# Half of the low weight parts made by ScalarE and an adding DMA instead of VectorE

## Chip, core and metric

The kernel runs on one core of one Trainium2 chip. The metric is the device time of one execution in microseconds; less is better. It is compared with the kernel before, timed on the same chip.

## What is computed

A trunk of two decoder layers over 256 tokens of width 2048, all in float32. Layer 0 mixes tokens with gated linear attention beside block attention, layer 1 with forgetting attention beside a gated recurrence. After each mixer comes an output projection and a wide MLP. Almost all arithmetic is in products of 256 rows with large weight matrices:

```python
u = rms_norm(h, norm_mix) @ w_in                    # 2048 x 6160 (layer 0), 2048 x 7176 (layer 1)
h = h + concat(mixer_a(u), mixer_b(u)) @ w_out      # 2048 x 2048
h = h + square(relu(rms_norm(h, norm_mlp) @ w_up)) @ w_down   # 2048 x 8192, 8192 x 2048
...
return rms_norm(h, final_norm)
```

## The kernel before

The big products are cut into blocks of 1024 output columns (a few of 1040 or 1032), and each block into 16 units. A unit is one weight tile of 128 rows by 1024 columns with the matmuls that use it. There are 784 units: 16 for each of 49 blocks (6 input, 2 output and 16 MLP blocks in layer 0; 7, 2 and 16 in layer 1).

TensorE multiplies in float32r, which keeps fewer bits than float32. So each operand is split in two: a high part, the value rounded to float32r, and a low part, what is left. `fetch(i)` prepares unit i: a load on SP's queue brings the raw tiles of two units at once (1 MB, line 972), ScalarE copies the raw tile into `wh` (line 978), and VectorE subtracts, `wl = raw - wh` (line 979). The raw tiles lie in three buffers of two units each (pool `wraw`); `wh` and `wl` have six buffers each, one per unit (pool `wspl`).

`step(t, i)` issues the six matmuls of unit i for token half t: activations high times `wh` (two banks), high times `wl` (two banks), low times `wh` (two banks), line 1006. The main loop runs over i: fetch(i + AHEAD), step(0, i), some background work of the mixers (transposes, small products, elementwise work, cut in pieces by `bg`), and step(1, i - LAG), with LAG = 2. A scheduler in the build may move instructions on an engine's queue as dependences allow; in the first 14 iterations `pin` holds the program's order. Each engine then works its own queue off in order, and the hardware waits only where a semaphore says so.

So the buffers of unit k become free when step(1, k - 6) has read them, which is in iteration k - 4. The first matmul of unit k is in iteration k. Between lie iterations k - 3, k - 2 and k - 1, whatever AHEAD is.

GpSimd has little work: masks, the reciprocal roots of the norms (lines 241 to 247) and a few copies. At the start it issues eight small loads (lines 142 to 147).

Of the kernel before, what the change touches and what calls it, by code (L numbers as in the profile page):

```python
# [8 lines left out]
F32 = mybir.dt.float32  # L9
# [11 lines left out]
LAG = 2  # L21
AHEAD = 2
STARTN = 14
# [14 lines left out]
def trunk(ctx: ExitStack, tc: tile.TileContext, x, ev_norm_mix, ev_w_in, ev_gla_gate_w2, ev_gla_gate_b,  # L38
# [10 lines left out]

# [1 line left out]
    # A task yields what its piece costs, or BAR: go on after the next step only.  # L51
    tasks = []
# [32 lines left out]

    # Buffers that tasks take and give back
    def aux():
# [22 lines left out]

# [1 line left out]
    h = cons.tile([P, 2, D], F32, name="h")  # L112
# [5 lines left out]

# [1 line left out]
    vrow0 = work.tile([16, P], F32, name="vrow0", tag="lev", bufs=NLEV)  # L120
# [41 lines left out]
    masks = {}  # L162
    # key - query distance, with the causal mask: columns [queries 0..127 | queries 128..255]
    dist = cons.tile([P, 384], F32, name="dist")
# [7 lines left out]
    def const_task():  # L172
        # tri[s, t] = 1 for s <= t < 128 and for t >= 128
        pool.memset(tri, 1.0)
        pool.affine_select(out=tri[:, 0:P], in_=tri[:, 0:P], pattern=[[1, P]], compare_op=ALU.is_ge, fill=0.0, base=0,
                           channel_multiplier=-1)
        pool.memset(seg, 1.0)
        pool.memset(seg.rearrange("p (a b) -> p a b", b=64)[:, :, 0:1], 0.0)
        for m in LEVELS[1:]:
            yield from room(0, 1)  # L180
            nb = 64 // m
            mf = lev()[:, 0:64]
            mk = cons.tile([P, 256], U8, name=f"mask{m}")
            mv = mf.rearrange("p (n m) -> p n m", m=m) if 1 < m < 64 else mf
            dims = [[2 * m, nb]] * (nb > 1) + [[0, m]] * (m > 1)
            pool.memset(mf, 1.0)
            pool.affine_select(out=mv, in_=mv, pattern=[[-a, b] for a, b in dims], compare_op=ALU.is_ge, fill=0.0,
                               base=0, channel_multiplier=1)
            pool.affine_select(out=mv, in_=mv, pattern=dims, compare_op=ALU.is_ge, fill=0.0, base=m - 1,
                               channel_multiplier=-1)  # L190
            yield BAR
            dve.tensor_copy(mk.rearrange("p (g c) -> p g c", c=64), mf.unsqueeze(1).to_broadcast([P, 4, 64]))
            lev_done()
            masks[m] = mk
            yield 0.3
        pool.iota(dist[:, 0:128], pattern=[[1, 128]], base=0, channel_multiplier=-1,
                  allow_small_or_imprecise_dtypes=True)
        pool.iota(dist[:, 128:384], pattern=[[1, 256]], base=-128, channel_multiplier=-1,
                  allow_small_or_imprecise_dtypes=True)
        causal(dist)  # L200
        yield BAR
        mx, e0, e1, sm = (small([P, 8], f"lb{i}", 1) for i in range(4))
        dve.tensor_tensor(mx, vec("lb0"), vec("lb1"), ALU.max)
        dve.tensor_sub(e0, vec("lb0"), mx)
        dve.tensor_sub(e1, vec("lb1"), mx)
        act.activation(e0, e0, AF.Exp)
        act.activation(e1, e1, AF.Exp)
        dve.tensor_add(sm, e0, e1)
        dve.reciprocal(sm, sm)
        dve.tensor_mul(e0, e0, sm)  # L210
        dve.tensor_mul(e1, e1, sm)
        dve.tensor_add(lb, e0, e1)
        dve.tensor_sub(lb, lb, e0)
        yield 1.0

# [1 line left out]
    xh = cons.tile([P, KT, S], F32R, name="xh")  # L217
# [9 lines left out]

# [1 line left out]
    ssq = {}  # L229
# [9 lines left out]
    def rsq(dst, v, n, scale):  # L239
        """dst = (v * scale + EPS) ** -0.5"""  # L240
        pool.tensor_scalar(dst, v, scale, EPS, ALU.mult, ALU.add)
        pool.tensor_tensor(dst, dst, mhalf[:, 0:n], ALU.pow)
# [8 lines left out]
    def pin(op):  # L251
        """In the first units each engine goes by the order of the program"""
        if state["start"]:
            tc.keep_in_program_order(op)
# [34 lines left out]

# [1 line left out]
    def evac_scaled(dst, acc, sc):  # L291
# [3 lines left out]
    def evac_extra(dst, accs, sc, extra, few, sf):  # L295
        """few <- the extra columns; dst <- the 1024 others"""
        a, b, c = accs
        n = 512 - extra
        m = n + b.shape[1]
        act.activation(dst[:, 0:n], a[:, extra:512], AF.Identity, scale=sc)  # L300
        dve.tensor_scalar(dst[:, n:m], b, sc, None, ALU.mult)
        dve.tensor_scalar(dst[:, m:1024], c, sc, None, ALU.mult)
        act.activation(few, a[:, 0:extra], AF.Identity, scale=sf)

    def silu_gen(z):
        """z = x / 2 -> x * sigmoid(x) = (1 + tanh(x / 2)) * x / 2"""
        for i in range(2):
# [9 lines left out]
    def heads_gen(src, n0, n, dst, t, func=AF.Copy, scale=1.0):  # L317
        """dst[:, 0:n, t] <- transposes of src's blocks n0.. (four at most)"""
        yield from room(1)
# [12 lines left out]

# [1 line left out]
    def spawn_scores(store, qT, kT, bT, escale, h0, diag, *needs):  # L334
        """Heads h0, h0+1. store[h0] = diag [key, (head tile), query], off [key, head, query].
        diag: [token, (head tile)] of q . k, if it's there already."""
        hs = slice(h0, h0 + 2)
# [100 lines left out]
    def gla_out(at, v, g, dv, h0, nh, k0, gain, halves, key):  # L438
        """Outputs of nh heads (nh * dv = 256) from head h0 on; k tiles k0, k0+1 of the half"""
        yield from room(1)  # L440
# [50 lines left out]

# [1 line left out]
    def soft_scores(pts, qT, kT, hd, bias_gen):  # L493
        """Leaves normalized probabilities, transposed [key, query]."""
        yield from room(2, 1)
# [59 lines left out]

# [1 line left out]
    class Block:  # L557
        def __init__(self, w, c0, rows, stat, evac, budget, ready, extra=0):
            """extra: so many columns before the 1024; the products are then in three banks."""
            self.w, self.c0, self.rows, self.stat, self.evac = w, c0, rows, stat, evac  # L560
# [3 lines left out]

# [1 line left out]
    def mixers(lay):  # L566
# [31 lines left out]

        # GLA
        def gla_qk(acc, t):  # L600
# [64 lines left out]

        # HGRN2
        def hg_q(acc, t):
# [5 lines left out]
            sg = stage()  # L673
            # the forget logits of FoX come with the queries
            evac_extra(sg, acc, st["rh"][:, t:t + 1], 8, st["fn"][:, t], st["r"][:, t:t + 1])
# [24 lines left out]
        def hg_gates():  # L700
            """e = exp(-z): log f = ln(1 + lb e) - ln(1 + e), k = 1 - f, b = running sums of log f"""
            b, k = st["b"], st["k"]
# [32 lines left out]

        # MoBA, FoX
        def soft_q(acc, t):
# [9 lines left out]
            else:  # L747
                # the low-rank gates of GLA come with the queries
                evac_extra(sg, acc, st["rq"][:, t:t + 1], 16, st["few"][:, t], st["r"][:, t:t + 1])
# [21 lines left out]
        def fox_forget():  # L771
            """ct = running sums of log sigmoid, token by token; nc = the same, negative, as rows"""
            z = st["fn"]
# [60 lines left out]
    def layer_blocks(lay):  # L834
# [17 lines left out]
        for half in range(2):  # L852
            # the stationary operands come mixer by mixer: its rows of the weights are order[j]
            bl.append(Block((w_out[0], order), half * CB, list(range(KT)), mstat, out_evac(half), 2.0, mready))
# [103 lines left out]

# [1 line left out]
    split, raws, accs = {}, {}, {}  # L960
    blocks, units = [], []

    def fetch(i):
# [14 lines left out]
        pin(act.activation(wh, raw, AF.Copy))  # L978
        pin(dve.tensor_sub(wl, raw, wh.bitcast(F32)))  # L979
        split[i] = (wh, wl)  # L980

    def step(t, i, end=None):
        """Step i, or steps i to end, the last ones of a block, bank by bank"""
        b, j = units[i]
# [17 lines left out]
        outs = list(zip(banks, b.cuts))  # L1002
        # bank by bank in the first and the last step, as the banks come and go one by one
        order = [(o, p) for o in outs for p in parts] if j in (0, n - 1) and i else [(o, p) for p in parts for o in outs]
# [6 lines left out]

    # first loads and transposes
    tk_const = Task(const_task())
# [68 lines left out]
```

## Time and profile before

| | |
|---|---|
| time, median of 2 runs | 2354.7 us (2353.91 to 2355.49) |
| span of the profiled execution, first to last instruction | 2351.9 us |
| what lies around the span, against that median | 2.8 us |
| TensorE matmul busy | 2333.3 us, 99% |
| VectorE busy | 1302.3 us, 55% |
| ScalarE busy | 1067.2 us, 45% |
| GpSimd busy | 61.7 us, 3% |
| read from HBM | 414.47 MB |

PE is TensorE's matmuls, PEld its weight loads, DVE VectorE, ACT ScalarE, POOL GpSimd, SP the engine that issues most loads; a name with q is an engine's queue of DMA issues. Busy time is the union of an engine's instructions. Matmuls overlap in the pipeline, so the sum of their single durations is more than the busy time.

### The profile page before, as it was taken

The page shows a single profiled execution, that of the slowest core. Times are in us where ns is not written, and L with a number is a line of the kernel's source. Part 1 is how long each engine was busy: PE and PEld are TensorE (multiplying, and loading weights), DVE is VectorE, ACT ScalarE, POOL GpSimd, SP SyncE. Part 2 cuts the span into 40 slices and gives each one's busy share as a digit, 9 for nine tenths or more (in the row PEclk, how much of TensorE's full clock was granted, in tenths as well). Part 3 has the DMA queues.
Part 4 walks back from the last instruction along what each step waited for, and adds up shares of the span by engine and source line. Part 5 has one row for each costly group of instructions (what it writes and reads, how often), then busy time and mean ns, then how long its engine had stood idle before and what let it go on. Part 6 is the DMA issues. An engine that isn't in the chain of part 4 may idle for free.

```text
span 2351.9 us, 27073 instructions
## 1 busy us (share of the span) xinstructions
PE 2333.3 (99%) x10836; PEld 1910.8 (81%) x10836; DVE 1302.3 (55%) x1595; ACT 1067.2 (45%) x1334; POOL 61.7 (3%) x126
## 2 busy tenths in 40 slices
PE   8999999999999999999999999999999999999998
PEld 7888888888888888888887888788888888888886
DVE  5485555554554554465557775555554554554554
ACT  5464544443443343344446455544443443443443
POOL 3000200000000000000000000100000000000000
PEclk9999999999999999999999999999999999999999
DMA  7545445555555555555554444455555555555553
GB/s 242 191 155 160 158 156 187 182 184 182 194 179 185 190 179 191 186 180 181 186 182 165 150 139 161 144 179 181 187 187 183 189 182 189 187 179 194 182 180 124
DMA packets 110590, 418.31 MB, mean 178 GB/s; under 512 B 6815, under 2 KB 8945, under 8 KB 110337
## 3 DMA queue, kind: packets, MB, share of 16 engines
q1 hardware_dynamic: 109536, 415.46, 53.6%
q8 instruction: 85, 1.39, 0.2%
q10 hardware_dynamic: 608, 1.06, 0.1%
q14 instruction: 41, 0.33, 0.0%
q0 software_dynamic: 320, 0.07, 0.0%
HBM read 414.47 MB, written 2.10 MB: 177 GB/s over the span
## 4 chain that ended last, share of the span: by engine, by line
PE 98%; DVE 1%; ACT 1%; DMA 0%; SPq 0%; issue 0%; POOL 0%; POOLq 0%; ACTq 0%
PE acc L1006 90%; PE aux L421 1%; PE aux L881 1%; PE aux L1006 1%; PE aux L260 1%; PE aux L322 1%; DMA raw<-in_ev_w_in_dram 0%; PE aux L499 0%; DVE hb L721 0%; PE aux L523 0%; PE aux L805 0%; ACT wh L978 0%; DVE wl L979 0%; PE aux L498 0%; PE aux L414 0%; PE aux L544 0%
## 5 line engine op out<-in xcount | busy, mean ns | idle before, releaser
L979 DVE TENSOR_TENSOR wl<-raw,wh 128x1024 fp32r<-128x1024 f32 (+2 forms) x784 | 959.7, 1225 | 919.2 <-ACT wh L978 918.8
L978 ACT ACTIVATE wh<-raw 128x1024 fp32r<-128x1024 f32 (+2 forms) x784 | 830.4, 1061 | 1169.3 <-PE acc L1006 1091.1
L1006 PE MATMUL acc<-wh,xh 128*128 128x512 f32 x1856 | 605.5, 396 | 2.5 <-ACT xh L266 2.5
L1006 PE MATMUL acc<-wl,xh 128*128 128x512 f32 x1856 | 591.8, 390 | 2.6 <-DVE wl L979 2.6
L1006 PE MATMUL acc<-wh,xl 128*128 128x512 f32 x1856 | 591.3, 389 | 0.0
L1006 PE MATMUL acc<-wh,mh 128*128 128x512 f32 x1280 | 418.2, 396 | 0.0
L1006 PE MATMUL acc<-wl,mh 128*128 128x512 f32 x1280 | 413.5, 394 | 0.0
L1006 PE MATMUL acc<-wh,ml 128*128 128x512 f32 x1280 | 412.9, 393 | 0.0
L1006 PEld LDWEIGHTS acc<-wl,xh 128*128 128x128 f32 x1856 | 344.9, 188 | 78.3 <-DVE wl L979 4.4
L1006 PEld LDWEIGHTS acc<-wh,xl 128*128 128x128 f32 x1856 | 345.3, 188 | 75.1
L1006 PEld LDWEIGHTS acc<-wh,xh 128*128 128x128 f32 x1856 | 339.0, 188 | 73.1 <-ACT xh L266 3.4
L1006 PEld LDWEIGHTS acc<-wl,mh 128*128 128x128 f32 x1280 | 240.5, 188 | 56.0
L1006 PEld LDWEIGHTS acc<-wh,ml 128*128 128x128 f32 x1280 | 240.3, 188 | 56.1
L1006 PEld LDWEIGHTS acc<-wh,mh 128*128 128x128 f32 x1280 | 239.0, 188 | 54.7 <-DVE h L843 1.5
L843 DVE TENSOR_TENSOR h<-acc,h 128x512 f32<-128x512 f32 x72 | 47.8, 685 | 21.0 <-PE acc L1006 21.0
L399 ACT ACTIVATE lev<-lev 128x512 f32<-128x512 f32 x48 | 29.8, 629 | 31.1 <-DVE lev L394 10.9
L875 DVE TENSOR_TENSOR stg<-stg 128x512 f32<-128x512 f32 x64 | 42.6, 686 | 2.4 <-ACT stg L866 1.5
L886 DVE TENSOR_TENSOR ml<-aux,mh 128x512 fp32r<-128x512 f32 x64 | 41.0, 682 | 0.0
L421 PEld LDWEIGHTS aux<-lev 128*128 128x128 f32 x288 | 36.7, 191 | 2.6
L881 PE MATMUL aux<-ident,stg 128*128 128x128 f32 x256 | 36.2, 274 | 0.0
L421 PE MATMUL aux<-lev 128*128 128x64 f32 x288 | 35.8, 269 | 0.0
L881 PEld LDWEIGHTS aux<-ident,stg 128*128 128x128 f32 x256 | 29.6, 140 | 6.6
(229 smaller groups left out, 862.4 us busy)
## 6 DMA issues: line engine op xcount, KB each, us to landing
raw<-in_ev_w_up_dram SPq DMA_DIRECT2D x64, 1024.0 KB, 5.1
raw<-in_ev_w_down_dram SPq DMA_DIRECT2D x64, 1024.0 KB, 5.1
raw<-in_od_w_up_dram SPq DMA_DIRECT2D x64, 1024.0 KB, 5.0
raw<-in_od_w_down_dram SPq DMA_DIRECT2D x64, 1024.0 KB, 5.1
raw<-in_od_w_in_dram SPq DMA_DIRECT2D x48, 1024.0 KB, 4.9
raw<-in_ev_w_in_dram SPq DMA_DIRECT2D x39, 1024.0 KB, 5.4
raw<-in_ev_w_out_dram SPq DMA_DIRECT2D x16, 1024.0 KB, 5.1
raw<-in_od_w_out_dram SPq DMA_DIRECT2D x16, 1024.0 KB, 5.1
```

What stands on the lines that cost most here:

```text
L260: pin(pe.transpose(ps[:, i * 256 + t * P:i * 256 + (t + 1) * P], h[:, t, kt * P:(kt + 1) * P], ident))
L322: pe.transpose(ps[:, i * P:(i + 1) * P], src[:, (n0 + i) * P:(n0 + i + 1) * P], ident)
L399: act.activation(e, e, AF.Exp, scale=escale)
L421: pe.matmul(ps[:, i * 64:(i + 1) * 64], a, r, start=True, stop=True)
L843: dve.tensor_tensor(h[:, t, sl], acc[i], h[:, t, sl], ALU.add)
L875: dve.tensor_tensor(sg[:, cs], sg[:, cs], sg[:, cs], ALU.mult)
L881: pe.transpose(ps[:, j * P:(j + 1) * P], sg[:, i * 512 + j * P:i * 512 + (j + 1) * P], ident)
L886: dve.tensor_sub(ml[:, ks, ts], pv, mh[:, ks, ts].bitcast(F32))
L978: pin(act.activation(wh, raw, AF.Copy))
L979: pin(dve.tensor_sub(wl, raw, wh.bitcast(F32)))
L1006: pin(pe.matmul(o, a, m[:, c0:c1], start=first, stop=last))
```

## The change

From unit 32 on, the units whose number leaves 2 or 3 when divided by 4 get their low part in another way. ScalarE writes `-raw`, rounded to float32r, into `wl`, and a DMA of GpSimd's queue then adds the raw tile to it. The subtraction on VectorE is left out for these units. There are 376 of them, always both units of one raw buffer, and the two units before and after stay as they were. AHEAD becomes 3. The number of buffers stays. All else in the diff are comments that became empty lines.

```diff
-AHEAD = 2
+AHEAD = 3
...
         wh = wspl.tile([P, n], F32R, name="wh", tag="wh")
         wl = wspl.tile([P, n], F32R, name="wl", tag="wl")
         pin(act.activation(wh, raw, AF.Copy))
-        pin(dve.tensor_sub(wl, raw, wh.bitcast(F32)))
+        if i >= 32 and i % 4 >= 2:
+
+            act.activation(wl, raw, AF.Copy, scale=-1.0)
+            pool.dma_start(out=wl, in_=raw, accum_op=ALU.add)
+        else:
+            pin(dve.tensor_sub(wl, raw, wh.bitcast(F32)))
         split[i] = (wh, wl)
```

## Rows read from the trace of the kernel before

**Rows 1.** The page's head and busy times.

```profile
span 2351.9 us, 27073 instructions
...
PE 2333.3 (99%) x10836; PEld 1910.8 (81%) x10836; DVE 1302.3 (55%) x1595; ACT 1067.2 (45%) x1334; POOL 61.7 (3%) x126
```

**Rows 2.** Who waited for whom, all engines: total us, times, longest.

```profile
ACT wh L978 <- PE acc L1006: 1091.1, 655, 5.2
POOL rstd L247 <- ACT stg L235: 997.6, 4, 726.8
...
ACT stg L866 <- PE acc L1006: 14.7, 16, 0.9
...
PEld acc L1006 <- DVE wl L979: 4.4, 4, 2.6
...
PE acc L1006 <- DVE wl L979: 2.6, 3, 2.1
```

**Rows 3.** The page's costliest groups: the two instructions of the split.

```profile
L979 DVE TENSOR_TENSOR wl<-raw,wh 128x1024 fp32r<-128x1024 f32 (+2 forms) x784 | 959.7, 1225 | 919.2 <-ACT wh L978 918.8
L978 ACT ACTIVATE wh<-raw 128x1024 fp32r<-128x1024 f32 (+2 forms) x784 | 830.4, 1061 | 1169.3 <-PE acc L1006 1091.1
```

**Rows 4.** Timeline of ScalarE near the end: start, duration, idle before and releaser.

```profile
2325.63 1.06 ACT L978 ACTIVATE wh<-raw 128x1024 fp32r<-128x1024 f32 x1 [1.73 <-PE acc L1006]
2328.41 1.06 ACT L978 ACTIVATE wh<-raw 128x1024 fp32r<-128x1024 f32 x1 [1.72 <-PE acc L1006]
```

**Rows 5.** Timeline of TensorE near the end.

```profile
2333.79 0.63 PE L1006 MATMUL acc<-wh,mh 128*128 128x512 f32 x2
2334.26 0.63 PE L1006 MATMUL acc<-wl,mh 128*128 128x512 f32 x2
```

**Rows 6.** Busy time by stage: stretch, length, busy times, clock, DMA share, GB/s.

```profile
0.00:300.00 300.00, 293.48 (x1474) 244.52 (x1475) 181.94 (x314) 159.05 (x241) 34.72 (x71) 1.00 0.56 180
300.00:392.00 92.00, 92.00 (x437) 75.83 (x436) 47.38 (x53) 41.80 (x53) 0.00 (x0) 1.00 0.53 172
392.00:1120.00 728.00, 728.00 (x3231) 591.83 (x3230) 386.97 (x384) 306.89 (x328) 1.11 (x3) 1.00 0.56 185
1120.00:1488.00 368.00, 365.57 (x1891) 304.72 (x1890) 232.89 (x371) 193.57 (x293) 20.31 (x38) 1.00 0.48 161
1488.00:1592.00 104.00, 104.00 (x496) 84.50 (x495) 53.83 (x79) 51.54 (x80) 2.97 (x8) 1.00 0.53 172
```

**Rows 7.** Timeline inside an MLP block: a split and what hands over.

```profile
700.98 1.06 ACT L978 ACTIVATE wh<-raw 128x1024 fp32r<-128x1024 f32 x1 [1.74 <-PE acc L1006]
...
702.08 1.22 DVE L979 TENSOR_TENSOR wl<-raw,wh 128x1024 fp32r<-128x1024 f32 x1 [1.57 <-ACT wh L978]
```

**Rows 8.** DMA issues: count, KB each, median us from issue to landing.

```profile
raw<-in_ev_w_up_dram SPq DMA_DIRECT2D x64, 1024.0 KB, 5.1
...
out_dram<-lev ACTq DMA_DIRECT2D x2, 256.0 KB, 2.8
...
vrow<-in_ev_norm_mlp_dram POOLq DMA_DIRECT2D x1, 8.0 KB, 6.1
...
fb<-in_od_fox_fgate_b_dram POOLq DMA_DIRECT2D x1, 4.0 KB, 5.0
```

**Rows 9.** GpSimd's groups: its own time for one DMA issue.

```profile
L147 POOL DMA_DIRECT2D fb<-in_od_fox_fgate_b_dram x1 | 0.6, 574 | 1.7 <-DMA vrow<-in_ev_norm_mlp_dram 1.7
```

**Rows 10.** DMA queues: packets, MB, share of the 16 engines' span.

```profile
q1 hardware_dynamic: 109536, 415.46, 53.6%
```

**Rows 11.** The loads of one matrix: duration of an issue, first and last start.

```profile
L972 SPq DMA_DIRECT2D raw<-in_od_w_down_dram x64: 367/368/368, 1685.2 to 2314.1; - x64
```

## The prediction

> **What bounds the kernel now.** I read the busy times first: TensorE's matmuls cover 2333.3 of 2351.9 us [rows 1], and the granted clock is 1.00 in every stage [rows 6]. So at most 18.6 us of the span are without a matmul, and no change that leaves the matmuls alone can give more. The view of waits says what little TensorE waits for: `wl` from VectorE costs it 2.6 us as a matmul and 4.4 us as a weight load, 7 us in all [rows 2]. ScalarE by contrast waits 1091.1 us, 655 times, to write `wh`, for a matmul to give the buffer back [rows 2]. The split is therefore early everywhere: it starts the moment a buffer is free. What counts is then how much time lies between that moment and the matmul that needs the result; nothing else of the change can reach the end of the kernel.
>
> **The cover.** Near the end two units can be followed by the order of the code. The last `wh` but one (unit 782) starts at 2325.63 [rows 4]. Counted back from the last matmul, step(0, 782) starts at 2333.79, and its first matmul with `wl` at 2334.26 [rows 5]. So a low part may be 2334.26 - 2325.63 = 8.63 us late against the start of its `wh` before TensorE stands still. An iteration takes 2328.41 - 2325.63 = 2.78 us there [rows 4], and the cover contains three, so where iterations are longer by d it is 8.63 + 3d. By stage [rows 6], length over units: MLP 728/256 = 2.84, cover 8.8 us; input blocks of layer 0 300/96 = 3.125, cover 9.7; of layer 1 368/112 = 3.29, cover 10.1; output blocks 92/32 = 2.9 and 104/32 = 3.25, cover 8.9 and 10.0. AHEAD does not enter: the buffers set the start, and there are still six. I take its rise to 3 at nothing.
>
> **What is removed.** 376 subtractions of 1.225 us [rows 3], 461 us of VectorE. It is 55% busy [rows 1], and TensorE waits for this line 7 us in all. The gain is between 0 and 7 us; I take 0, as most of these waits may be in the first units.
>
> **What ScalarE gets.** 376 ACTIVATEs like that of `wh`, 1.06 us each [rows 3]: 399 us more. In the MLP its load goes from 307 to 307 + 128 x 1.06 = 443 of 728 us [rows 6], 61%. It stays off the end as an engine. A block's evacuation (line 866) could queue behind one of them: ScalarE now stands ready for it up to 0.9 us early [rows 2]. If all 29 blocks that ScalarE evacuates lost 0.7 us, it would be 20 us; a step of the other half (half an iteration, 1.4 us) lies between an evacuation and the next use of its bank, so I take 0.
>
> **What GpSimd gets.** 376 DMA issues, at 0.57 us each of its own time [rows 9] some 215 us beside 62 us of work [rows 1]. Each waits for ScalarE's `-raw`, and behind it in the queue stand the reciprocal roots. Those of the norms run 4 times after long waits [rows 2] and have most of a block of 16 units before their first use; the masks, copies and roots of the mixers are background work. Cost 0; with that cover gone, some ten such waits of an iteration, 2.8 us, are 28 us.
>
> **The adding DMA, the term that decides.** No such DMA is in the trace. From the start of `wh` to the landed `wl` I add:
> - `wh` and `-raw`, 2 x 1.06 us [rows 3] = 2.12
> - hand-over to the next engine, as 702.08 - 700.98 - 1.06 [rows 7] = 0.04
> - issue to landing of a DMA of GpSimd's queue with next to no bytes: 5.0, the 4 KB one over 128 partitions, at a time when loads were under way [rows 8]
> - the bytes. It reads two tiles of 512 KB, as much as one load reads. From 256 KB in 2.8 us to 1024 KB in 5.1 us [rows 8] is 2.3 us for 768 KB, so 3.1 for 1 MB.
>
> Sum 10.3 us, against a cover of 8.8 in the MLP. Lower end: the bytes of one tile at that slope, with the start of the other queues (2.8 + 0.8 = 3.6), sum 5.8, hidden. Upper end: 6.1 for the start [rows 8], twice the bytes' time because a load shares the engines, sum 14.4. I take 10.3, since the row of the same queue with 128 partitions is the nearest.
>
> The Trainium skill speaks for less: DMA: Bandwidth & Descriptors, section "Anatomy of one DMA — SWDGE (gpsimd) path", puts the fixed part of a GpSimd DMA at about 2.0 us. The trace's tiny ones took 5.0 to 6.1. An estimate by that page, 2.0 + 3.1, would make the sum 7.3 us and the change free, which is the first rival below.
>
> **What a late low part costs.** Units 2 and 3 of each four are late, 0 and 1 are not. TensorE's stand for unit 2 also delays the point from which unit 3 is needed, and it is itself inside the three iterations that unit 3 of the four before has as cover. So each four units lose (sum - cover) once. There are 188 fours: 128 in the MLP, 16 and 28 in the input blocks, 8 and 8 in the output blocks.
> - MLP 128 x 1.5 = 192
> - input blocks 16 x 0.6 + 28 x 0.2 = 15
> - output blocks 8 x 1.4 + 8 x 0.3 = 14
>
> Together 221 us, on the profiled execution's 2351.9 + 2.8 us around it = 2354.7, which is the median of the runs: **2576 us**. At the upper end of 14.4 us it is 128 x 5.6 + 16 x 4.7 + 28 x 4.3 + 8 x 5.5 + 8 x 4.4 = 992, so 3346.
>
> **Loads.** A raw buffer whose units are added by DMA is given back at 10.3 instead of 2.3 us after the start of `wh`. The last load was issued at 2314.1 [rows 11], lands 5.1 us later [rows 8], and its first `wh` is at 2325.63 [rows 4]: 6.4 us early. With three buffers the late one goes to the next two units that VectorE serves, and those have 8.8 - 2.3 = 6.5 us of cover beside. 8.0 us fit in 12.9: no cost.
>
> **Rivals.**
> 1. *Hidden (not slower).* If the DMA lands within 6.6 us of its issue (8.8 - 2.16), TensorE never waits and the time is 2355, with the gains and losses above 2345 to 2375. For it: 256 KB from another queue need 2.8 us [rows 8], and the scheduler may put the step of the other half ahead of the matmuls that wait, which adds up to 1.4 us of cover. Against: the 5.0 to 6.1 us of GpSimd's tiny DMAs. Up to 0.35 us of loss per four units it still counts as no change, since 2% (47 us), about what a measurement of this kernel can tell, is reached there.
> 2. *The DMA engines become the bound.* In the MLP they are busy 0.56 of 11.4 us per four units [rows 6], 6.4 us; 5.0 are left. Two adding DMAs are 256 rows, 16 for each engine, so a row may take 0.31 us. A packet of a load takes 0.536 x 16 x 2351.9 / 109536 = 0.184 us [rows 10]; with two reads 0.37, so 5.9 us: full, though less than the stand in my sum. At 0.55 us a row (three packets' worth) four units need 15.2 us: 128 x 3.8 = 486, and worked out alike 158 in the other stages, make **2999 us**. For it: the share is high already. Against: SBUF is both ends, and nothing shows an addition to cost more than its reads. The Trainium skill holds with reads as the price: Collectives: The Full Stack, section "The bandwidth ceiling: the fold count and why AG ≠ RS ≠ AR", says a reducing transfer runs at half rate because of the second read. No run here shows it yet; by it the engines are about full, which is why this rival gets a quarter.
> 3. *Faster.* VectorE's relief could give 7 us, the whole idle time 18.6: under 1%.
>
> **How the numbers follow.** My forecast (late by 0.35 to 3 us in the MLP, 2400 to 2860) gets 0.45; hidden 0.28; DMA engines as the bound 0.26; faster by over 2% 0.01. So faster 0.01, same 0.28, slower 0.71. The range goes from the small gain, 2345, up to 3000: it holds the forecast, the hidden case and about half of the second rival.
>
> **What would show it.** If I am right: TensorE's waits name the DMA into `wl` (or what ScalarE does before it), with some 1.5 us a time, about 128 to 190 times, in units 2 and 3 of each four; its clock stays 1.00; the DMA's issue to landing reads about 8 us; VectorE falls to about 840 us, ScalarE rises to about 1466. If the landing reads under 6.6 us and TensorE stays at 99%, the first rival holds. If the DMA share nears 1 and loads land late too, the second. The prediction fails if the start of a GpSimd DMA is not the 5 us taken, or if an added row costs far from two packets.

## The result and the profile after

The changed kernel takes 2817.02 us (median of two runs, 2814.84 to 2819.19) against 2354.7: a ratio of 1.196, with a 95% interval of 1.194 to 1.199. The forecast was slower by 221 us; it is slower by 462. The direction and the place came as forecast. The size is twice as large, and a part of it, matmuls that take longer, was not in the forecast at all.

The head and the busy times of the page after, with GpSimd's DMA queue, answer to [rows 1] and [rows 10]:

```profile
span 2817.5 us, 28606 instructions
...
PE 2475.1 (88%) x10836; PEld 1972.3 (70%) x10836; DVE 856.3 (30%) x1219; ACT 1422.5 (50%) x1710; POOL 380.6 (14%) x502
...
q1 hardware_dynamic: 109536, 415.46, 47.7%
q0 software_dynamic: 54464, 197.26, 35.3%
```

The span grew by 2817.5 - 2351.9 = 465.6 us, and two differences on TensorE make it up. Its time without a matmul rose from 18.6 to 2817.5 - 2475.1 = 342.4 us (+323.8). And the same 10836 matmuls cover 2475.1 instead of 2333.3 us (+141.8). The view of waits says whom it stands for (us in total, times, longest), answering to [rows 2]:

```profile
ACT wl L981 <- PE acc L1011: 735.2, 326, 7.7
...
PEld acc L1011 <- DMA wl<-raw: 397.3, 177, 4.8
PE acc L1011 <- DMA wl<-raw: 323.6, 157, 4.4
...
ACT wh L978 <- DMA raw<-in_od_w_down_dram: 57.4, 26, 3.0
```

The adding DMA is the only large one: 323.6 us as a matmul, 2.06 us a time, 157 times for 188 groups of four units. (The weight loads' 397.3 us are mostly the same stands, seen by the loads ahead of those matmuls.) ScalarE starts `-raw` late too, but only because it waits for the buffer, as before.

The group of GpSimd's issues (its own time, mean ns), and the issue-to-landing medians, which answer to [rows 8, 9]:

```profile
L982 POOL DMA_DIRECT2D wl<-raw x376 | 323.9, 862 | 2274.3 <-ACT wl L981 2162.4 <-ACT wh L978 48.8 <-PE acc L1011 36.0
```

```profile
wl<-raw POOLq DMA_DIRECT2D x368, 512.0 KB, 10.0
raw<-in_ev_w_up_dram SPq DMA_DIRECT2D x64, 1024.0 KB, 7.9
...
raw<-in_od_w_down_dram SPq DMA_DIRECT2D x64, 1024.0 KB, 9.6
```

The add takes 10.0 us to land, and a load that took 5.1 now takes 6 to 10. One group of four units can be followed in the timeline inside an MLP block (start, duration, operation; in brackets the idle time before it and its releaser; first ScalarE and the queues, then TensorE):

```profile
704.98 1.06 ACT L981 ACTIVATE wl<-raw 128x1024 fp32r<-128x1024 f32 x1 [2.87 <-PE acc L1011]
705.39 0.88 SPq L972 DMA_DIRECT2D raw<-in_ev_w_up_dram  x2
705.94 1.04 ACT L978 ACTIVATE wh<-raw 128x1024 fp32r<-128x1024 f32 x1
706.33 0.86 POOL L982 DMA_DIRECT2D wl<-raw  x1 [9.10 <-ACT wl L981]
709.10 0.86 POOL L982 DMA_DIRECT2D wl<-raw  x1 [1.91 <-ACT wl L981]
...
716.74 1.22 PE L1011 MATMUL acc<-wl,xh 128*128 128x512 f32 x2 [2.59 <-DMA wl<-raw]
717.76 1.06 PE L1011 MATMUL acc<-wh,xl 128*128 128x512 f32 x2
718.61 1.06 PE L1011 MATMUL acc<-wh,xh 128*128 128x512 f32 x2
...
719.25 0.88 SPq L972 DMA_DIRECT2D raw<-in_ev_w_up_dram  x2
```

Three things are to be seen. `-raw` runs ahead of `wh`, and the DMA goes out 706.33 - 704.98 = 1.35 us after its start. TensorE reaches the matmul that needs the result at 716.74 - 2.59 = 714.15, so the cover is 9.2 us; 1.35 + 10.0 = 11.35 us is 2.1 us too late, about the mean wait (in this group TensorE stands for 2.59 us). And within 3.7 us two loads (in one pair of issues) and two adds go out; then no load and no add until 719.25, 13.9 us after the first pair, where it begins again. The same stretch by windows of 3 us (stretch, length, busy times of TensorE's matmuls and weight loads, VectorE, ScalarE and GpSimd, granted clock, DMA share, GB/s):

```profile
704.00:707.00 3.00, 3.00 (x15) 2.43 (x14) 0.00 (x0) 2.01 (x2) 0.67 (x1) 1.00 0.48 86
707.00:710.00 3.00, 3.00 (x15) 2.44 (x14) 0.00 (x0) 2.01 (x2) 1.05 (x2) 1.00 0.94 295
710.00:713.00 3.00, 3.00 (x15) 2.45 (x14) 0.52 (x1) 1.06 (x1) 0.00 (x0) 1.00 0.98 276
713.00:716.00 3.00, 1.15 (x6) 0.60 (x4) 1.82 (x2) 1.06 (x1) 0.00 (x0) 1.00 1.07 276
716.00:719.00 3.00, 2.26 (x5) 1.84 (x6) 0.10 (x1) 0.00 (x0) 0.00 (x0) 0.54 0.82 165
719.00:722.00 3.00, 3.00 (x13) 2.44 (x12) 0.00 (x0) 1.77 (x2) 0.42 (x1) 0.89 0.54 132
```

The DMA engines swing between half idle and full. An estimate from the queues' rows above: two loads are 512 packets of 0.477 x 16 x 2817.5 / 109536 = 0.196 us, 6.3 us for 16 engines, and two adds are 256 rows of 0.331 us (worked out below), 5.3 us. These 11.6 us of work begin at 705.39, and the stand ends at 716.74.

In the window from 716 on the granted clock is 0.54, close to the 1.2 GHz level, and a pair of matmuls takes 718.61 - 717.76 = 0.85 us from start to start, where it took 0.47 [rows 5]. Slow matmuls are a second part of the loss, beside the stand itself. But not every stand is followed by them. After one of 2.52 us, some 56 us later, the next window reads 1.00:

```profile
772.50 0.73 PE L1011 MATMUL acc<-wl,xh 128*128 128x512 f32 x2 [2.52 <-DMA wl<-raw]
```

```profile
773.00:776.00 3.00, 3.00 (x14) 2.42 (x14) 0.00 (x0) 1.34 (x2) 0.00 (x0) 1.00 0.46 92
```

Over the span the mean clock is 0.960. With two levels, half speed then held for some 2 x 0.040 x 2817.5 = 225 us, which makes matmuls at most 113 us longer (an estimate). So at least 28 of the 141.8 us are something else, which no run isolates.

### The profile page after: what moved, and what is told of

Same layout as the page of the kernel before. It is cut to its first block, busy times and chain, and to the rows that moved or that the text cites. A ratio compares the mean times of both kernels' runs of the same rounds, so it can differ in the third digit from the quotient of the medians.

```text
span 2817.5 us, 28606 instructions
## 1 busy us (share of the span) xinstructions
PE 2475.1 (88%) x10836; PEld 1972.3 (70%) x10836; DVE 856.3 (30%) x1219; ACT 1422.5 (50%) x1710; POOL 380.6 (14%) x502
## 3 DMA queue, kind: packets, MB, share of 16 engines
q1 hardware_dynamic: 109536, 415.46, 47.7%
## 4 chain that ended last, share of the span: by engine, by line
DMA 59%; PE 27%; issue 9%; ACT 3%; SPq 1%; POOL 1%; DVE 0%; POOLq 0%; ACTq 0%
DMA wl<-raw 36%; PE acc L1011 23%; DMA raw<-in_ev_w_up_dram 5%; DMA raw<-in_od_w_down_dram 5%; DMA raw<-in_ev_w_down_dram 4%; DMA raw<-in_od_w_up_dram 4%; DMA raw<-in_ev_w_in_dram 2%; ACT wl L981 2%; DMA raw<-in_od_w_in_dram 1%; DMA raw<-in_od_w_out_dram 1%; PE aux L421 1%; SPq L972 1%; PE aux L1011 0%; DMA raw<-in_ev_w_out_dram 0%; ACT wh L978 0%
## 5 line engine op out<-in xcount | busy, mean ns | idle before, releaser
L984 DVE TENSOR_TENSOR wl<-raw,wh 128x1024 fp32r<-128x1024 f32 (+2 forms) x408 | 499.6, 1226 | 1504.4 <-ACT wh L978 1502.8
L981 ACT ACTIVATE wl<-raw 128x1024 fp32r<-128x1024 f32 (+1 forms) x376 | 398.2, 1059 | 776.7 <-PE acc L1011 735.2
L1011 PE MATMUL acc<-wl,xh 128*128 128x512 f32 x1856 | 617.3, 404 | 154.5 <-DMA wl<-raw 154.4
L982 POOL DMA_DIRECT2D wl<-raw x376 | 323.9, 862 | 2274.3 <-ACT wl L981 2162.4
L1011 PE MATMUL acc<-wh,xl 128*128 128x512 f32 x1856 | 605.3, 398 | 0.0
L1011 PE MATMUL acc<-wl,mh 128*128 128x512 f32 x1280 | 444.7, 420 | 169.4 <-DMA wl<-raw 169.2
L1011 PE MATMUL acc<-wh,mh 128*128 128x512 f32 x1280 | 437.0, 412 | 0.0
L1011 PE MATMUL acc<-wh,ml 128*128 128x512 f32 x1280 | 433.8, 411 | 0.0
L1011 PEld LDWEIGHTS acc<-wh,ml 128*128 128x128 f32 x1280 | 254.6, 199 | 60.9
L867 DVE TENSOR_SCALAR stg<-acc,rstd 128x512 f32<-128x512 f32 x32 | 23.9, 747 | 80.6 <-PE acc L1011 80.6
```

Of the source, the lines that this page charges most:

```text
L867: dve.tensor_scalar(sg[:, 512:1024], acc[1], r, 0.0, ALU.mult, ALU.max)
L981: act.activation(wl, raw, AF.Copy, scale=-1.0)
L982: pool.dma_start(out=wl, in_=raw, accum_op=ALU.add)
L1011: pin(pe.matmul(o, a, m[:, c0:c1], start=first, stop=last))
```

## The experiments

Every edit is made to the changed kernel. Times are one run each unless a ratio is given; the kernel before ran beside them at 2354 to 2355 us.

**ScalarE's part alone (e11).** ScalarE writes `-raw` as in the change, with AHEAD = 3, and VectorE adds the raw tile:

```
-            pool.dma_start(out=wl, in_=raw, accum_op=ALU.add)
+            dve.tensor_tensor(wl, raw, wl.bitcast(F32), ALU.add)
```

> ScalarE writes -raw as in the change, and VectorE adds the raw tile in place of the DMA (the low part is the same): ScalarE's 399 us and AHEAD = 3 alone, with no DMA. All theories that blame the DMA: 2355 to 2365 us. If ScalarE's extra work or the order on its queue costs: 2400 us and more.

2355.31 us. ScalarE's added work (1423.0 us busy, against 1067.2 before) and AHEAD cost nothing; the whole loss hangs on the DMA.

**More cover (e1, e4).** e1 sets LAG from 2 to 1, so that the two halves' steps of a unit lie closer and its buffers come free sooner. e4 issues the older unit's step ahead of the newer one's:

```
-LAG = 2
+LAG = 1
```

```
+        if LAG <= i < total:
+            step(1, i - LAG)
         ...  step(0, i)
-        if LAG <= i < total:
-            step(1, i - LAG)
```

> The change with LAG = 1 in place of 2: the second token half follows one iteration behind, so the six buffers of wl come free one iteration (2.8 us) earlier. Theory A (the low part is late against the cover that the buffers give): the cover grows from 9.2 to about 12 us, the adding DMA needs 11.4 to 11.8 us from the free buffer, so TensorE's waits for it fall from 324 us to under 40, its clock goes back to 1.00, and the time is 2355 to 2400 us. Theory B (the DMA engines, 83% busy, are the bound): more cover buys nothing, the time stays above 2650 us.

> The change with step(1, i - LAG) issued before step(0, i) in the loop: half an iteration, 1.4 us, of TensorE's own work stands ahead of the matmuls that wait. Theory A: each wait of 2.06 us on average falls to 0.7 us or less, the half-clock stretches mostly go too, and the time is 2400 to 2550 us. Theory B: no change, 2800 us.

e1: 2728.7 us, ratio 1.162 (1.156 to 1.169). e4: 2740.2. Waits of e1:

```profile
PEld acc L1011 <- DMA wl<-raw: 213.7, 120, 4.9
PE acc L1011 <- DMA wl<-raw: 163.0, 93, 4.5
...
ACT wh L978 <- DMA raw<-in_ev_w_down_dram: 121.7, 30, 8.6
...
ACT wl L981 <- DMA raw<-in_ev_w_down_dram: 96.8, 28, 4.9
```

TensorE's wait for the add is halved, as the theory of cover says, but 2355 to 2400 us were expected, and only some 90 of 462 us come back. In its place ScalarE now stands for loads: 887 us over all rows of that kind, against 209.5 in the change. A second limit lies just behind the first: a load, the split, the add that still reads the raw tile, and only then the next load into that buffer. e4, expected at 2400 to 2550 us, shows the same.

**The trip through the raw buffers alone (e2), with a fourth buffer (e6), and the same adds onto nothing (e5).** In e2 VectorE makes every low part; the DMA adds `wh` onto the raw tile behind it, so it has the size and the place of the change's and holds the raw buffer, but TensorE needs none of it. e6 gives it four raw buffers, and for the room five pairs of split tiles and LAG = 1. In e5 the DMA adds `wh` onto one of two spare tiles (LAG = 1, five pairs too): nothing waits for it but the next use of `wh` and of the spare tile.

```
-            act.activation(wl, raw, AF.Copy, scale=-1.0)
-            pool.dma_start(out=wl, in_=raw, accum_op=ALU.add)
+            dve.tensor_sub(wl, raw, wh.bitcast(F32))
+            pool.dma_start(out=raw, in_=wh.bitcast(F32), accum_op=ALU.add)                  # e2, e6
+            pool.dma_start(out=junk[i % 2][:, 0:n], in_=wh.bitcast(F32), accum_op=ALU.add)  # e5
```

> VectorE makes every low part, as before, but the same 376 adding DMAs of 512 KB run, onto the raw tile (raw plus wh, after both halves are made; nothing reads the sum). They hold the raw buffer back as in the change, and nothing that TensorE reads waits for them. Theory A: the time is that of before, 2355 to 2375 us, though the DMA engines carry the same bytes. Theory B (traffic, late loads or GpSimd's issues cost the time): 2600 us and more.

> VectorE makes every low part, and the 376 adding DMAs of 512 KB (wh onto two spare tiles that nothing reads) hold neither a raw buffer nor anything that TensorE waits for. To make room LAG is 1 and wspl has five buffers, which leaves the cover of the change. Theory C (the loop through the three raw buffers: a load waits for the adding DMA that gives the buffer back, and both have become slow): with the raw buffers free the time is 2355 to 2400 us. Theory B (the DMA engines cannot carry the bytes in the time): 2700 us and more, as with the traffic that held the raw buffers (2760).

> The traffic of the second experiment (adding DMAs onto the raw tiles, VectorE makes all low parts) with a fourth raw buffer, for which LAG = 1 and five buffers in wspl make room. Theory C: a fourth buffer adds two units, 5.7 us, to each trip of a raw buffer, and the time falls from 2760 to 2360 to 2450 us. Theory B: no change, 2700 us and more.

e2: 2759.9 us, ratio 1.172 (1.169 to 1.175). e6: 2485.0. e5: 2356.8, no loss. Busy times, queues and landings of e5:

```profile
PE 2335.0 (99%) x10836; PEld 1912.5 (81%) x10836; DVE 1302.8 (55%) x1595; ACT 1068.3 (45%) x1334; POOL 386.7 (16%) x504
...
q1 hardware_dynamic: 109536, 415.46, 49.0%
q0 software_dynamic: 54464, 197.26, 45.9%
...
junk<-wh POOLq DMA_DIRECT2D x368, 512.0 KB, 6.6
raw<-in_ev_w_up_dram SPq DMA_DIRECT2D x64, 1024.0 KB, 7.5
```

This is the run that decides between the forecast and its second rival. The same loads and the same 376 adds fit into 2355 us, with the engines at 49.0 + 45.9 = 95% of the span; taken over the span, their rate is enough. What costs is who waits for a landing. In e2 that is only the raw buffer's next load, and it alone costs 405 us, with what the clock lost (0.944 on average); e6, with a fourth buffer, has 275 less of it, somewhat short of what was expected. Waits of e2:

```profile
ACT wh L978 <- DMA raw<-in_ev_w_down_dram: 256.4, 50, 10.9
ACT wh L978 <- DMA raw<-in_od_w_down_dram: 231.0, 46, 10.1
```

**A fourth raw buffer in the change itself (e12).**

```
-LAG = 2          wraw ... bufs=3    wspl ... bufs=6
+LAG = 1          wraw ... bufs=4    wspl ... bufs=5
```

> The change with four raw buffers; LAG = 1 and five buffers in wspl make room, so the cover of the low part is that of the change. If the direct lateness of the low part is most of the loss (theory A): TensorE's waits for the DMA stay at 300 us and the time at 2700 to 2820 us. If the trip through three raw buffers is most of it (theory C): loads are early again and the time is 2400 to 2550 us.

2824.0 us, no better than the change. With five pairs and LAG = 1 the cover is about that of six and LAG = 2, and TensorE waits as there:

```profile
PE acc L1011 <- DMA wl<-raw: 326.7, 158, 4.3
```

So at the change's own cover it is the low part's lateness that sets the time, and late loads are only the next limit. (The loads of e12 still leave in pairs, as in the change, and its adds land in 10.0 us too.)

**Why 10 us: the addition (e3).** A plain copy in place of the adding one (so these low parts are the whole raw tile):

```
-            pool.dma_start(out=wl, in_=raw, accum_op=ALU.add)
+            pool.dma_start(out=wl, in_=raw)
```

> The change with a plain copy of the raw tile in place of the addition (the low part is then the whole raw tile, so the output is another): same queue, same bytes written, one read of 512 KB in place of two. If the second read sets the price: a row takes about 160 ns and not 327, the landing falls from 10.0 to 6 to 7 us, under the cover of 9.2 less 1.35, and the time to 2355 to 2420 us. If the start of a GpSimd DMA sets it (5 us, as I forecast), the landing stays at 8 to 9 us and the time at 2500 to 2700 us.

2438.7 us, just above the range. Its queue, its landing and TensorE's wait:

```profile
q0 software_dynamic: 54464, 197.26, 22.0%
...
wl<-raw POOLq DMA_DIRECT2D x368, 512.0 KB, 6.9
```

```profile
PE acc L1011 <- DMA wl<-raw: 63.0, 63, 2.1
```

The 376 x 128 = 48128 rows take 0.220 x 16 x 2437.0 / 48128 = 0.178 us each, against 0.353 x 16 x 2817.5 / 48128 = 0.331 in the change (all of the queue's time put down to them). The addition makes a row 1.86 times as dear and the landing 3 us longer, and without it 378 of the 462 us are gone. That its second read is the reason fits the factor, but no run parts the read from the adding.

**Why 10 us: the company (e7, e9, e8).** e7 takes units 1 and 3 of each four instead of 2 and 3, so that the two adds go out apart. e9 takes unit 3 alone, half of the adds. e8 puts six idle matmuls (on a spare bank) ahead of the first `wl` matmul of nearly each adding unit: TensorE works where it stood.

```
-        if i >= 32 and i % 4 >= 2:
+        if i >= 32 and i % 2 == 1:      # e7
+        if i >= 32 and i % 4 == 3:      # e9
```

```
+            if fill and m is split[i][1]:       # e8
+                junk = aux()
+                for r in range(6):
+                    pe.matmul(junk, sh[:, ts], split[i][0][:, 0:512], start=True, stop=True)
```

> The change with the adding DMAs spread: units 1 and 3 of each four in place of 2 and 3. The same count and the same bytes, never two in a row, but now every raw buffer is held by one. Theory A (lateness of the low part alone): the landing falls below 10 us since no two overlap, and the time falls to 2500 to 2700 us. Theory C (raw buffers): two trips of a raw buffer, each some 22 us with load, split and add, against 34 us for the twelve units between: 2900 us or more. Theory B: 2817 us, the same bytes.

> The change with the adding DMA for unit 3 of each four alone (188 in place of 376). Theory D (in the change the two loads and the two adds of four units all go out within some 4 us, since the hold of one raw buffer by its adds brings the free times of two buffers together; 10.3 us of work for the DMA engines then lie in one burst, and the landing is 10 us though the engines idle between bursts): the burst is 5.1 us of loads and 2.6 of adds, the landing falls to 7 to 8 us, with 1.35 us ahead of it that is about the cover of 9.2 us, and the time is 2355 to 2450 us. Theory A with a fixed landing: one late unit costs each four units as much as two, 2750 to 2820 us.

> The change with six idle matmuls of 512 columns (1.4 us, into a spare PSUM bank, read by nobody) in the first half-step of each unit that waits, ahead of the matmuls that need the adding DMA. They lie in time in which TensorE stood still (2.06 us a wait on average). If the fall of TensorE's clock to 0.96 on average costs time by itself: the clock goes to 0.99 or more, the 142 us that the busy time of the same matmuls rose by mostly go, and the time is 2700 to 2760 us. If the clock costs nothing, since a faster TensorE only waits longer for the DMA: 2810 to 2830 us. If the filler is simply more work: up to 2950 us.

e7: 2504.1 us. e9: 2361.8. e8: 2874.8. One line of each page, the landing:

```profile
wl<-raw POOLq DMA_DIRECT2D x368, 512.0 KB, 6.6
```

```profile
q0 software_dynamic: 27392, 98.67, 21.7%
...
wl<-raw POOLq DMA_DIRECT2D x184, 512.0 KB, 5.4
```

```profile
PE 2844.7 (99%) x13032; PEld 2322.8 (81%) x13032; DVE 858.4 (30%) x1219; ACT 1426.8 (50%) x1710; POOL 382.0 (13%) x502
...
wl<-raw POOLq DMA_DIRECT2D x368, 512.0 KB, 6.8
```

An add lands in 5.4 us where only one goes out for each four units (e9), in 6.6 where two go out apart (e7), in 10.0 in the change. That the change's two adds follow each other is not the reason by itself. In e5 they do so too, 2.8 us apart as in the change, and land in 6.6; but there the loads go out one at a time:

```profile
707.02 0.37 SPq L975 DMA_DIRECT2D raw<-in_ev_w_down_dram  x1
708.79 0.86 POOL L985 DMA_DIRECT2D junk<-wh  x1 [7.46 <-ACT wh L981]
711.57 0.86 POOL L985 DMA_DIRECT2D junk<-wh  x1 [1.91 <-ACT wh L981]
712.56 0.37 SPq L975 DMA_DIRECT2D raw<-in_ev_w_down_dram  x1
```

e9 loses 7 us in all: 1.35 + 5.4 us is well within the cover, so the first rival's case exists, but with half of the adds. e7's median of 6.6 would fit too; single landings reach 10.3, and TensorE still waits 98.2 us for it, 93 times. e8 was to separate the slow clock from the wait and doesn't: it adds 13032 - 10836 = 2196 matmuls, 2196 x 0.235 = 516 us (an estimate from the 0.47 of a pair), more than it could save. But it shows two things. With 14 waits left of 157 and the clock at 0.999, the kernel's own matmuls are back at about 2844.7 - 516 = 2329 us, so the added 142 us hang on the stands. And in nearly the same span as the change's, with the same bytes but without the stands, the adds land in 6.8 us. The 10 us belong to the rhythm of stand and burst, not to the number of bytes.

**e7 with LAG = 1 (e10).**

> Spread adds (units 1 and 3 of each four) and LAG = 1, which adds 2.8 us of cover. Both causes taken together, bunching and too little cover: the landing stays near 6.6 us, TensorE's waits for the low part go from 98 to 146 us to under 20, and the time is 2355 to 2400 us. If the raw buffers, each now held by an add, are a bound of their own: 2450 to 2550 us, with ScalarE waiting for loads.

2434.0 us, ratio 1.033 (1.028 to 1.038), between the two forecasts: the best version with all 376 adds in use, 79 us above before. TensorE hardly waits for a low part any more; ScalarE waits for loads:

```profile
ACT wh L978 <- DMA raw<-in_od_w_down_dram: 155.9, 55, 5.5
ACT wh L978 <- DMA raw<-in_ev_w_down_dram: 140.8, 51, 5.8
...
PE acc L1011 <- DMA wl<-raw: 8.0, 10, 2.4
```

**What makes the burst (e13, e14).** In the change the loads leave in pairs, as a raw buffer held by its adds and the one after it come free almost together. e13 lets the add read `wh` instead of `raw` (the low part of these units is then zero); the raw tile is then free as early as in the kernel before. e14 puts the loads that wait for an add on GpSimd's queue, so that others needn't queue behind them on SP's:

```
-            pool.dma_start(out=wl, in_=raw, accum_op=ALU.add)
+            pool.dma_start(out=wl, in_=wh.bitcast(F32), accum_op=ALU.add)      # e13
```

```
-                nc.sync.dma_start(raws["cur"], ...)
+                q = pool if i >= 38 and (i - 6) % 4 >= 2 else nc.sync          # e14
+                q.dma_start(raws["cur"], ...)
```

> The change with the adding DMA reading wh in place of raw: the same queue, bytes and place, TensorE still waits for it, but the raw buffer is free when ScalarE has read it twice, not when the DMA has landed. The low part comes out as zero for these units, so the low part of half the weights is left out of the result. It waits for wh as well, which ScalarE writes after -raw, so 1 us later than in the change. Theory D (the hold of the raw buffer makes the loads go out in pairs, into the adds): loads go out singly, the landing falls from 10.0 to 6.5 to 7 us, and with 2.3 us ahead of it it is about the cover of 9.2: 2355 to 2450 us. If the hold does not matter (two adds close together beside any loads take 10 us): 2817 us or, for the 1 us, up to 3000.

> The change with the loads that must wait for adds (into buffers held by them) on GpSimd's queue; SP's queue has the other loads alone, so that none stands behind a load that waits. If SP's order makes the pairs: one load goes out 2.5 us earlier than now, the landing falls to 7 to 9 us and the time to 2500 to 2700 us. If both buffers come free so close together that the queue does not matter: landing 9.5 to 10.5 us, 2750 to 2850 us.

e13: 2781.1 us. Its loads leave singly again, and its landing falls:

```profile
wl<-wh POOLq DMA_DIRECT2D x368, 512.0 KB, 8.1
raw<-in_ev_w_up_dram SPq DMA_DIRECT2D x64, 1024.0 KB, 5.8
```

But the DMA must now wait for `wh` too and goes out 2.3 instead of 1.35 us after the start: 10.4 us in all, still over the 9.2. e14: 2716.5 us, landing 9.2, between its two forecasts. So the held raw buffers make about 2 of the 3.4 us between 6.6 and 10.0 (in e13 the two adds also go out further apart, 6.67 and 3.68 us in its timeline from 705 to 725). The rest is not explained by a run. That TensorE's stand gathers the buffers' releases, and so the next loads and adds, into one burst fits the timeline, e5 and e8, but is only argued.

No version beats the kernel before, whose TensorE is 99% busy.

## Why the prediction was right in kind and half in size

Wrong were the price of the landing and the term that was put at nothing, TensorE's clock. Of the 465.6 - 221 = 245 us that the forecast lacked, the longer stands are 324 - 221 = 103 and the longer matmuls 142 (the clock at most 113 of them).

- *What bounds the kernel, and that the cover counts:* right. e11 costs nothing, e5 costs nothing, and with a shorter landing (e9) the loss is all but gone. That nothing else can reach the end of the kernel is too strong: the hold of the raw buffers can (e2).
- *The cover:* 8.8 us forecast in the MLP, 9.2 measured in the group shown. ScalarE takes `-raw` ahead of `wh`, so the two ACTIVATEs and the hand-over before the issue are 1.35 us, not 2.16. Both errors were in the change's favour, 1.2 us together.
- *The landing, the term that failed:* 8.1 us forecast, 10.0 measured, and wrong in both of its parts. "Issue to landing of a DMA of GpSimd's queue with next to no bytes: 5.0" is no start: from e9, 5.4 us less 8 rows at 0.217 x 16 x 2360.1 / 24064 = 0.34 leaves 2.7, and the shortest landings of the change, 4.5 us, and of e3, 2.9 us, leave 1.8 and 1.5 in the same way (estimates). Those tiny DMAs went out while loads were under way, as the prediction itself noted; whether that made them slow, no run shows. The bytes were priced at 3.1 us by rows of the kernel before, where the loads go out one at a time; they take the other 7.3 (10.0 - 2.7, an estimate) where two adds and two loads go out together. The errors partly cancel, which is luck: it is why 10.3 stood near the 11.35 of the change. The stands, forecast at 1.5 us each in the MLP, were 2.06 us on average: 324 us instead of 221.
- *"Its clock stays 1.00":* wrong, and worth more than the first error. The clock was 0.960 on average, 0.54 in the window shown, and the matmuls cover 142 us more. Stands and longer matmuls together are (323.8 + 141.8) / 157 = 2.97 us for each stand. The clock can make at most 113 of the 142; e3, with 63 waits and the clock at 0.998, also has 2356.7 - 2333.3 = 23 us more. How much would come back by itself if only the clock held was not measured, as e8 couldn't tell.
- *One loss for four units:* right, 157 stands for 188 groups.
- *VectorE's relief, AHEAD, ScalarE's and GpSimd's own time at nothing:* right (e11, e5), though GpSimd's issue takes 0.86 us, not 0.57.
- *"Loads ... no cost":* right for the change (e12), but for the wrong reason: 8.0 us do not fit easily when loads need 6 to 10 us and the add 10. The hold costs 405 us by itself (e2), and more cover alone brings the time no lower than 2729 and 2740 us (e1, e4), with ScalarE waiting for loads.
- *The first rival, hidden:* right that it needs about 6.6 us; half of the adds reach that. Where the Trainium skill (DMA: Bandwidth & Descriptors, section "Anatomy of one DMA — SWDGE (gpsimd) path") puts the fixed part of such a DMA at about 2.0 us, this case's 1.5 to 2.7 (estimates, from e3, the change and e9) are much nearer to it than the 5.0 that I took.
- *The second rival, the engines' rate:* a row costs 0.33 us, somewhat under the 0.37 of two reads and far from 0.55. Over the whole span the share did not hold the time up (e5), although 2817 stands nearer to that rival's 2999 than to the forecast; within a burst the engines are full (0.94 to 1.07 from 707 to 716). The Trainium skill (Collectives: The Full Stack, section "The bandwidth ceiling: the fold count and why AG ≠ RS ≠ AR") has a reducing transfer among cores run at half rate for its second read. The factor of 0.331 to 0.178 in e3 agrees; the reason was not tested here.

## What to carry to other kernels

When a step moves from a compute engine to a DMA, compare the landing, in the company of whatever is issued in the same few microseconds, with the time from buffer free to first use; the queue's mean share says little about it (95% busy and free in e5, 83% and 462 us in the change). When the sum is over the cover, count what the stands do to TensorE's clock as well as the stands. A DMA that reads a load's buffer also holds that buffer, and ties the next load to its landing.

## What the runs showed that was not expected

- A 512 KB adding DMA lands in 5.4, 6.6, 8.1 or 10.0 us (medians of e9, e7, e13, the change), and in 4.5 to 12.2 within the change.
- A stand of 2.59 us was followed by a granted clock of 0.54 over the next 3 us, and of 0.89 over the 3 us after that; one of 2.52 us was not.
- DMA engines that are 95% busy over the whole span cost TensorE nothing (e5), and slowed loads from 5.1 to 7.5 us.
